# A fp32 decoder trunk: the last output product of an FFN chunk in two halves, no short products, and unused products in TensorE's first two stops

## The chip, the cores and the metric

The kernel runs on one core of one Trainium2 chip. The metric is the device time of one execution in microseconds (us). TensorE (PE) multiplies and loads its stationary operand with a separate instruction (PEld in the rows); VectorE is DVE, ScalarE is ACT, GpSimd is POOL, and SyncE (SP) issues the DMAs.

## The reference

Two layers over 256 tokens of width 1024 in float32: a recurrent layer with an FFN, then shared keys and values and an attention layer with an FFN.

```python
for layer in range(DEPTH):
    if layer < N_A_LAYERS:
        h = h + recurrent_block(h, ...)        # z = rmsnorm(h) @ w_in; conv, gates, scan; @ w_out
    else:
        if layer == N_A_LAYERS:
            shared = shared_kv(h, ...)
        h = h + nsa_layer(h, ..., *shared)
    h = h + swiglu(h, f_norm[layer], f_w_in[layer], f_w_out[layer])

def swiglu(h, norm_g, w_in, w_out):
    u = rmsnorm(h, norm_g)
    gu = u @ w_in
    return (jax.nn.silu(gu[..., :FFN_HIDDEN]) * gu[..., FFN_HIDDEN:]) @ w_out
```

FFN_HIDDEN is 2816.

## The kernel before

Every large product is done in three: each operand is split into a high part and a low part, and `mm3` adds high x high, high x low and low x high into one PSUM bank. Weights come as a stream of 512 KB tiles (`raw`). ACT casts a tile to its high part `wh`, then DVE (now and then POOL) subtracts to get the low part `wl`; when `wl` is written, SP issues the load of the tile four places later.

**The opening.** The order of work in the recurrent layer is written out by hand in `PLAN_A`: each word runs one step of a named piece. PE first runs three unused products (`warm_up`, into the bank `wps`) and a broadcast of the norm's gain (g). `norm_rows` (na) makes a normalised token block on ACT, POOL and DVE; `norm_tr` (nt) transposes it on PE (ntpa), eight 128x128 transposes for each of the two token blocks, and ACT and DVE split the result into `uah` and `ual`. Then come the projections z, each of 24 products of 256 columns: eight with `wh` and `uah`, eight with `wl`, eight with `ual`. `conv` (c) turns each z into a row block X on DVE, whose queue also holds the short steps of `decay` (sp, word d).

**The FFN.** `ffn` works through eleven chunks of 256 hidden units. Chunk 0 is done token-major in `in_mm`. For the chunks 1 to 10 `in_fm(c)` computes gate and up (f0g and f0u; f1g and f1u in the second layer) from four weight tiles, with 256 tokens as moving columns: 96 products of 128x256. `act_fm` makes the hidden values, and `out_both(c-1)` adds the chunk before to the four output banks accf: 2 weight tiles x 2 token blocks x 2 column halves x 3 = 24 products of 128x512. The last two chunks' outputs are done in `out_mm`. So PE goes from 512-column to 256-column products at the start of each `in_fm`, ten times a layer, and there `in_fm` has one product more, `T.matmul(ps[0][:, 0, :LEAD[layer]], ...)`, with 64 columns in the first layer and 96 in the second. The real first product starts its bank anew, so nothing reads it. By the order of instructions it is also the one that waits for ACT's `wh`.

Of the kernel before, what the change touches and what calls it, by code (L numbers as in the profile page):

```python
# [18 lines left out]
P = 128  # L19
# [3 lines left out]
NT = S // P  # L23
# [33 lines left out]

WARM = 3, 0

LEAD = 64, 96  # L60

PLAN_A = """
na0tA na0G na0 na0 nt0A na1 na1 e0t nt0 na1G na1t nt0 nt0tV nt0 w0A nt1a nt1G nt1 nt1a nt0a e0 nt1t nt1 w1 w1 w2 w3
w2V w0G z0V c0 d0 d0 d0 d0 c0 d0G d0 c0G d0 d0A w3G c0 z1 d0 d0 d0 c1 c1 c1a c1G d0 d0 d0 d0 z2 d0V d0a d0 w4 g0 g0 w4
g1G g1 g1 d0 d0 c2 c2 c2 d0 d0 d0 g0 d0 c2 d0 d0 d0 d0 z3 c3 d0 w5 g2 d0 d0 g2 g2 d0 d0 c3a c3A d0 c3 w6 z4 w6 c4 g3
g3 w7 d0V d0 g3 d0A d0 d0 d0 w5G d0 c4 d0 d0 c4 c4 w7 z5 g4 g4 g4 d0 d0 d0 d0 d0 d0 d0 d0 c5 c5 c5 d0 l0 w8 w8G z6 d0
# [150 lines left out]
def hybrid_trunk(ctx: ExitStack, tc: tile.TileContext, x, wsrc, gatew, gains, vecs, cvec, hvec, rope_c, rope_cc,  # L217
                 masks, sel, posT, w2d, out):
    nc = tc.nc
    V, A, T, GP = nc.vector, nc.scalar, nc.tensor, nc.gpsimd  # L220
# [11 lines left out]
    def bank(tag, name):  # L232
        tag = {"m": "mm", "a": "acc", "t": "tp"}.get(on.bank, tag)
        return psum.tile([P, 512], F32, tag=tag, name=name, bufs={"mm": 2, "acc": 4, "tp": 2}[tag])

    def gain(i):
        g = work.tile([P, D], F32, tag="gain", name=f"gain{i}", bufs=1)
        nc.sync.dma_start(g, gains[i:i + 1, :].broadcast_to([P, D]))
        return g[:, 0:512], g[:, 512:1024]
# [13 lines left out]
    for t in range(NT):  # L253
        for i in range(2):
            c = slice(i * 512, (i + 1) * 512)
# [9 lines left out]
    wps = bank("mm", "warmps").rearrange("p (a b) -> p a b", b=P)[:, 0:2]  # L265
# [10 lines left out]
    ident = msk[:, 0:128]  # L276
# [14 lines left out]
    def tok(a, k, t):  # L291
        return a[:, k, t * P:(t + 1) * P]

    def u_tiles(nm, use="m"):
        return [work.tile([P, KT, S], F32R, tag=f"{use}{c}", name=f"u{c}{nm}", bufs=1) for c in "hl"]

    def acc_pair(nm):
        return [bank("acc", f"acc{nm}_{n}") for n in range(2)]
# [42 lines left out]
            V.tensor_tensor(ul, pv, f32v(uh), ALU.subtract)  # L341
            yield

    def mm3(ps, ah, al, bh, bl, start, stop):

        T.matmul(ps, ah, bh, start=start, stop=False)  # L346
        T.matmul(ps, ah, bl, start=False, stop=False)  # L347
        T.matmul(ps, al, bh, start=False, stop=stop)  # L348


    ap = ExitStack()
# [19 lines left out]
    ab, e, z, z2, acc, r0, c2, nc2 = (sp[:, i, :] for i in range(8))  # L371

    def decay():

        V.tensor_scalar(z, e, 2.0, None, ALU.add)
        yield
        V.reciprocal(r0, z)
        yield
        V.tensor_tensor(z, e, r0, ALU.mult)
        yield  # L380
        V.tensor_tensor(z2, z, z, ALU.mult)
        yield
        V.tensor_scalar(acc, z2, 1.0 / 17.0, None, ALU.mult)
        yield
        for k in (15, 13, 11, 9, 7, 5, 3):
            V.scalar_tensor_tensor(acc, acc, 1.0 / k, z2, ALU.add, ALU.mult)
            yield
        V.scalar_tensor_tensor(acc, acc, 1.0, z, ALU.add, ALU.mult)
        yield
        V.tensor_scalar(r0, lam, -1.0, 0.0, ALU.mult, ALU.max)  # L390
        yield
        V.scalar_tensor_tensor(acc, acc, 2.0, r0, ALU.mult, ALU.add)
        yield
        V.tensor_scalar(c2, acc, 2.0, None, ALU.mult)
        yield
        V.tensor_scalar(nc2, acc, -4.0, None, ALU.mult)
        yield

    def consts():
# [70 lines left out]
    def proj_k(t, base, ah, al, ps, k):  # L470
        h, lo = W.parts[base + k]
        for n in range(2):
            c = slice(n * 512, (n + 1) * 512)
            mm3(ps[n], tok(ah, k, t), tok(al, k, t), h[:, c], lo[:, c], k == 0, k == KT - 1)
# [16 lines left out]
    def a_gain():  # L491
        gf0.append(gain(1))
        u0.extend(u_tiles("f0"))
        yield

    do = {
        "na": lambda t: norm_rows(t, g0, f"a{t}"), "nt": lambda t: norm_tr(t, (uah, ual), f"a{t}"), "e": lambda _: consts(),
        "d": lambda _: decay(), "w": lambda *n: W.pieces(), "z": z_mm, "c": conv, "g": gates, "l": lru, "y": y_out,
        "o": a_proj, "r": a_res, "nf": a_tr, "gf": lambda _: a_gain(),
    }  # L500
    play(PLAN_A, do, on)
    ap.close()
# [3 lines left out]
    def ffn(layer, u, wi, mid, fin, more=None):  # L506
# [3 lines left out]
        acc = [None, None]  # L510
# [4 lines left out]
        def in_base(c):  # L515
            return wi if c == 0 else wi + 4 + 6 * (c - 1)

        def out_base(c):
            return in_base(c + 1) + 4 if c < FC - 1 else end - 2

        def in_mm(t, c, late=None):
            ps = bank("mm", f"f{layer}i{t}_{c}")
            for k in range(KT):
                if late and k == KT - 1:
                    late()
                h, lo = W.get(in_base(c) + k // 2)
                s = slice((k % 2) * 512, (k % 2 + 1) * 512)
                mm3(ps, tok(u[0], k, t), tok(u[1], k, t), h[:, s], lo[:, s], k == 0, k == KT - 1)
            return ps
# [11 lines left out]
        def tr(t, c):  # L541
            pt = bank("tp", f"f{layer}t{t}_{c}")[:, :256]
            hd = hid.pop((t, c))
            for k in range(2):
                T.transpose(pt[:, k * P:(k + 1) * P], hd[:, k * P:(k + 1) * P], ident)
            if c not in hT:
                hT[c] = parts(c)
            hh, hl = (tok(m, slice(0, 2), t) for m in hT[c])
            pv = pt.rearrange("p (k q) -> p k q", k=2)
            A.copy(hh, pv)  # L550
            V.tensor_tensor(hl, pv, f32v(hh), ALU.subtract)

        def in_fm(c, between=()):

            tag = "mm" if c % 2 else "tp"
            ps = [bank(tag, f"f{layer}{x}_{c}").rearrange("p (k s) -> p k s", k=2) for x in "gu"]
            for j in range(4):
                h, lo = W.get(in_base(c) + j)
                if j == 0:
                    T.matmul(ps[0][:, 0, :LEAD[layer]], h[:, :P], u[0][:, 0, :LEAD[layer]], start=True, stop=True)  # L560
                for k in range(KT):
                    s = slice(k * P, (k + 1) * P)
                    mm3(ps[j // 2][:, j % 2], h[:, s], lo[:, s], u[0][:, k], u[1][:, k], k == 0, k == KT - 1)
                if j < len(between):
                    between[j]()
            return ps
# [28 lines left out]
        def out_both(c):  # L595
            if c == 0:
                for t in range(NT):
                    acc[t] = acc_pair(f"f{layer}_{t}")
            hh, hl = hT.pop(c)
            for k in range(2):  # L600
                h, lo = W.get(out_base(c) + k)
                for t in range(NT):
                    for n in range(2):
                        s = slice(n * 512, (n + 1) * 512)
                        mm3(acc[t][n], tok(hh, k, t), tok(hl, k, t), h[:, s], lo[:, s], c == 0 and k == 0, False)


        with tc.manual_schedule():
            ps = in_mm(0, 0, mid)
            act(0, 0, ps)  # L610
            W.split(wi + 6)
            ps = in_mm(1, 0)
            act(1, 0, ps)
        for c in range(1, FC - 1):
            W.split(in_base(c) + 4)
            ps = in_fm(c, [lambda: tr(0, 0), lambda: tr(1, 0)] if c == 1 else ())
            act_fm(c, ps)
            out_both(c - 1)
            if c == 1 and more:
                more()  # L620
        c = FC - 1
        W.split(end)
        ps = in_fm(c)
        act_fm(c, ps)
        for t in range(NT):
# [15 lines left out]
    w2 = pt1.tile([P, 2, 2, HD], F32, name="w2")  # L641
# [34 lines left out]
    ps = {}  # L676
# [567 lines left out]
```

## Time and profile before

| | us |
|---|---|
| median of 3 runs | 627.31 (627.07 to 627.53) |
| the profiled execution | 628.81 |
| its span, first to last instruction | 626.8 |
| PE busy | 611.4 (98%) |
| PE loading stationary operands | 548.2 (87%) |
| DVE busy | 407.7 (65%) |
| ACT busy | 327.0 (52%) |
| POOL busy | 117.9 (19%) |

The durations of single instructions overlap on PE: products are pipelined, and a product of 0.39 us may be followed by the next after 0.23. What a product costs in a run is therefore the step from its start to the next one's start. The clock column is the granted share of TensorE's full speed; an idle time in square brackets is that of the engine before the row, with what ended it.

### The profile page before, as it was taken

The numbers are of one execution on the slowest core, as the hardware profiler recorded it, in microseconds if no ns is written. First come the engines' busy times: TensorE is split into PE (matmuls) and PEld (weight loads), VectorE is DVE, ScalarE is ACT, GpSimd is POOL, SyncE is SP. The second block draws the span as 40 slices with busy tenths as digits, with TensorE's granted clock in tenths as the row PEclk, the third lists the DMA queues.
The fourth block names the chain that finished last, engine by engine and source line by source line (L and its number), as shares of the span: only waits on it lengthen the run. The fifth ranks groups of instructions, "written<-read, shape, count | busy, mean of one in ns | idle before, by whom it ended". The sixth has DMA issues, their size and how long they took to land.

```text
span 626.8 us, 10483 instructions
## 1 busy us (share of the span) xinstructions
PE 611.4 (98%) x4087; PEld 548.2 (87%) x4087; DVE 407.7 (65%) x630; ACT 327.0 (52%) x598; POOL 117.9 (19%) x133
## 2 busy tenths in 40 slices
PE   6999899999999999999999999999999999999997
PEld 4899777999999999988999886777899999999996
DVE  5879957755555555559776788888665555555542
ACT  6489656554444444452545578764554444444440
POOL 4223021210000000000446758754100000000000
PEclk8999999999999999999999999999999999999999
DMA  7444563875555655535545340333476666656622
GB/s 274 170 137 167 174 229 122 276 267 195 198 186 187 201 191 185 197 103 182 172 134 183 121 135 7 116 115 106 133 265 202 187 189 198 194 183 196 199 70 67
DMA packets 31380, 106.75 MB, mean 170 GB/s; under 512 B 4014, under 2 KB 5730, under 8 KB 31203
## 3 DMA queue, kind: packets, MB, share of 16 engines
q1 hardware_dynamic: 31331, 106.08, 52.0%
q8 instruction: 32, 0.52, 0.3%
q14 instruction: 17, 0.14, 0.1%
HBM read 105.02 MB, written 1.05 MB: 169 GB/s over the span
## 4 chain that ended last, share of the span: by engine, by line
PE 84%; DVE 7%; ACT 4%; DMA 3%; issue 2%; SPq 0%; DVEq 0%; ACTq 0%
PE accf L348 6%; PE accf L347 6%; PE accf L346 6%; PE f0g L346 3%; PE f1g L346 3%; PE f0g L347 3%; PE f1u L346 3%; PE f0g L348 3%; PE f1g L347 3%; PE f1g L348 3%; PE f0u L347 3%; PE f0u L346 3%; PE f0u L348 3%; PE f1u L347 3%; PE f1u L348 3%; DMA raw<-in_wsrc_dram 3%
## 5 line engine op out<-in xcount | busy, mean ns | idle before, releaser
L204 DVE TENSOR_TENSOR wl<-raw,wh 128x1024 fp32r<-128x1024 f32 x148 | 181.3, 1229 | 137.0 <-ACT wh L143 137.0
L143 ACT CAST wh<-raw 128x1024 fp32r<-128x1024 f32 x161 | 168.1, 1051 | 176.4 <-issue 38.8
L347 PE MATMUL accf<-wl,fhh 128*128 128x512 f32 x176 | 68.6, 390 | 0.0
L348 PE MATMUL accf<-wh,fhl 128*128 128x512 f32 x176 | 68.5, 389 | 0.0
L346 PE MATMUL accf<-wh,fhh 128*128 128x512 f32 x176 | 68.5, 389 | 0.0
L204 POOL TENSOR_TENSOR wl<-raw,wh 128x1024 fp32r<-128x1024 f32 x16 | 40.2, 2518 | 44.1 <-ACT wh L143 20.5
L346 PE MATMUL f0g<-uhf,wh 128*128 128x256 f32 x160 | 45.3, 283 | 0.0
L346 PE MATMUL f1g<-uhf,wh 128*128 128x256 f32 x160 | 45.0, 281 | 0.0
L347 PE MATMUL f0g<-ulf,wh 128*128 128x256 f32 x160 | 44.3, 277 | 0.0
L346 PE MATMUL f0u<-uhf,wh 128*128 128x256 f32 x160 | 44.3, 277 | 0.0
L346 PE MATMUL f1u<-uhf,wh 128*128 128x256 f32 x160 | 44.3, 277 | 0.0
L348 PE MATMUL f0g<-uhf,wl 128*128 128x256 f32 x160 | 44.2, 277 | 0.0
L347 PE MATMUL f1g<-ulf,wh 128*128 128x256 f32 x160 | 44.2, 276 | 0.0
L348 PE MATMUL f1g<-uhf,wl 128*128 128x256 f32 x160 | 44.2, 276 | 0.0
L347 PE MATMUL f0u<-ulf,wh 128*128 128x256 f32 x160 | 44.2, 276 | 0.0
L347 PE MATMUL f1u<-ulf,wh 128*128 128x256 f32 x160 | 44.2, 276 | 0.0
L348 PE MATMUL f0u<-uhf,wl 128*128 128x256 f32 x160 | 44.2, 276 | 0.0
L348 PE MATMUL f1u<-uhf,wl 128*128 128x256 f32 x160 | 44.2, 276 | 0.0
L348 PEld LDWEIGHTS accf<-wh,fhl 128*128 128x128 f32 x176 | 33.0, 188 | 7.0
L347 PEld LDWEIGHTS accf<-wl,fhh 128*128 128x128 f32 x176 | 33.0, 188 | 6.2
L346 PEld LDWEIGHTS accf<-wh,fhh 128*128 128x128 f32 x176 | 33.0, 188 | 6.2
L1019 ACT ACTIVATE pr<-s,sm 128x128 f32<-128x128 f32 (+1 forms) x64 | 26.2, 424 | 9.7 <-DVE sm L1013 6.9
(315 smaller groups left out, 1508.2 us busy)
## 6 DMA issues: line engine op xcount, KB each, us to landing
raw<-in_wsrc_dram SPq DMA_DIRECT2D x184, 512.0 KB, 4.2
raw<-in_wsrc_dram SPq DMA_DIRECT2D x8, 544.0 KB, 4.4
hres<-in_x_dram SPq DMA_DIRECT2D x4, 256.0 KB, 3.2
gw<-in_gatew_dram SPq DMA_DIRECT2D x1, 1024.0 KB
gain<-in_gains_dram SPq DMA_DIRECT2D x2, 512.0 KB, 7.0
out_dram<-hres SPq DMA_DIRECT2D x8, 128.0 KB, 1.8
tab<-in_hvec_dram SPq DMA_DIRECT2D x1, 256.0 KB, 5.0
tab<-in_rope_c_dram SPq DMA_DIRECT2D x1, 128.0 KB, 3.9
```

The costliest lines, as they stand in the source:

```text
L143: self.nc.scalar.copy(dst, src)
L204: self.on.pick(nc.gpsimd if i in LOW_ON_POOL else nc.vector).tensor_tensor(lo[:, :w], t[:, :w], f32v(h[:, :w]), ALU.subtract)
L346: T.matmul(ps, ah, bh, start=start, stop=False)
L347: T.matmul(ps, ah, bl, start=False, stop=False)
L348: T.matmul(ps, al, bh, start=False, stop=stop)
L1019: A.activation(pr[:, h1 + i, br], sv[:, br], AF.Exp, bias=sm[:, 0, h0 + i, br:br + 1], accum_out=sm[:, 1, h0 + i, br:br + 1])
```

## The change

Three edits. `LEAD` and the unused product in `in_fm` are gone. `mm3` can issue its third product (low x high) in two halves of 256 columns, and `out_both` asks for that in the last of its eight `mm3` (k = 1, last token block, second column half). A new piece `fill` (word wm) issues unused products into `wps`; the plan has two of them behind the first block's transposes and three behind the second's. `ident` is the 128x128 identity that the transposes use.

```diff
-LEAD = 64, 96
-
 PLAN_A = """
-na0tA na0G na0 na0 nt0A na1 na1 e0t nt0 na1G na1t nt0 nt0tV nt0 w0A nt1a nt1G nt1 nt1a nt0a e0 nt1t nt1 w1 w1 w2 w3
+na0tA na0G na0 na0 nt0A na1 na1 e0t nt0 wm2 na1G na1t nt0 nt0tV nt0 w0A nt1a nt1G wm3 nt1 nt1a nt0a e0 nt1t nt1 w1 w1 w2 w3
...
-    def mm3(ps, ah, al, bh, bl, start, stop):
+    def mm3(ps, ah, al, bh, bl, start, stop, halves=False):
...
-        T.matmul(ps, al, bh, start=False, stop=stop)
+        for i in range(2 if halves else 1):
+            c = slice(i * 256, (i + 1) * 256) if halves else slice(0, ps.shape[-1])
+            T.matmul(ps[:, c], al, bh[:, c], start=False, stop=stop)
...
+    def fill(n):
+
+        for _ in range(n):
+            T.matmul(wps, ident, ident[:, None, :].to_broadcast([P, 2, P]), start=True, stop=True)
+        yield
...
-        "o": a_proj, "r": a_res, "nf": a_tr, "gf": lambda _: a_gain(),
+        "o": a_proj, "r": a_res, "nf": a_tr, "gf": lambda _: a_gain(), "wm": fill,
...
-                if j == 0:
-                    T.matmul(ps[0][:, 0, :LEAD[layer]], h[:, :P], u[0][:, 0, :LEAD[layer]], start=True, stop=True)
...
-                        mm3(acc[t][n], tok(hh, k, t), tok(hl, k, t), h[:, s], lo[:, s], c == 0 and k == 0, False)
+                        ops = acc[t][n], tok(hh, k, t), tok(hl, k, t), h[:, s], lo[:, s], c == 0 and k == 0, False
+                        mm3(*ops, halves=(k, t, n) == (1, NT - 1, 1))
```

PE's queue before, from the end of one `out_both` to the start of the next `in_fm` (accf are the output banks, wh and wl the weight tile's parts, fhh and fhl the hidden values' parts, uhf and ulf the input's parts):

```order
504 L346 MATMUL accf_1_1_1310<-wh_1531,fhh_1_1293 128x512
505 L347 MATMUL accf_1_1_1310<-wl_1532,fhh_1_1293 128x512
506 L348 MATMUL accf_1_1_1310<-wh_1531,fhl_1_1294 128x512
507 L560 MATMUL f0g_1573<-uhf_867,wh_1549 128x64 [waits Activation_49]
508 L346 MATMUL f0g_1573<-uhf_867,wh_1549 128x256
509 L347 MATMUL f0g_1573<-ulf_868,wh_1549 128x256
```

and the same place after the change:

```order
504 L345 MATMUL accf_1_1_1314<-wh_1535,fhh_1_1297 128x512
505 L346 MATMUL accf_1_1_1314<-wl_1536,fhh_1_1297 128x512
506 L349 MATMUL accf_1_1_1314<-wh_1535,fhl_1_1298 128x256 x2
507 L345 MATMUL f0g_1578<-uhf_872,wh_1554 128x256 [waits Activation_49]
508 L346 MATMUL f0g_1578<-ulf_873,wh_1554 128x256
```

The 64-column product is gone, its wait on ACT has moved to the first real f0g product, and the last accf product stands as two of 256 columns.

PE's queue before in the opening, from the gain's broadcast to the first z (msk holds the identity, xna the normalised tokens):

```order
3 L274 MATMUL g_101<-grow,zero 128x512
4 L334 MATMUL ntpa_0_133<-msk,xna_126 128x128 x4
5 L334 MATMUL ntpa_1_134<-msk,xna_126 128x128 x4
6 L334 MATMUL ntpa_0_160<-msk,xna_140 128x128 x4
7 L334 MATMUL ntpa_1_161<-msk,xna_140 128x128 x4
8 L417 MATMUL z_194<-uha,wh_157 128x256 x8
```

and after the change:

```order
3 L272 MATMUL g_101<-grow,zero 128x512
4 L332 MATMUL ntpa_0_133<-msk,xna_126 128x128 x4
5 L332 MATMUL ntpa_1_134<-msk,xna_126 128x128 x4
6 L403 MATMUL warmps<-msk 128x256 x2
7 L332 MATMUL ntpa_0_162<-msk,xna_140 128x128 x4
8 L332 MATMUL ntpa_1_163<-msk,xna_140 128x128 x4
9 L403 MATMUL warmps<-msk 128x256 x3
10 L424 MATMUL z_199<-uha,wh_159 128x256 x8
```

Two unused products stand behind the first block's transposes and three behind the second's. The queues of ACT, DVE, POOL and SP are as before.

## Rows read from the trace of the kernel before

**Rows 1.** The page: the chain that ended last, shares of the span

```profile
PE 84%; DVE 7%; ACT 4%; DMA 3%; issue 2%; SPq 0%; DVEq 0%; ACTq 0%
```

**Rows 2.** Both FFNs' stretches, in order: length, busy of PE, PEld, DVE, ACT, POOL; clock; DMA

```profile
109.00:264.00 155.00, 155.00 (x1148) 146.40 (x1148) 85.93 (x98) 71.85 (x98) 6.20 (x16) 1.00 0.63 209
...
452.00:623.00 171.00, 171.00 (x1241) 160.21 (x1239) 89.63 (x108) 73.59 (x101) 0.00 (x0) 1.00 0.58 180
```

**Rows 3.** The opening by stretches, columns as in rows 2

```profile
6.14:7.18 1.04, 0.00 (x1) 0.04 (x1) 1.04 (x2) 0.63 (x3) 0.28 (x2) 1.00 0.99 179
...
8.25:9.30 1.05, 0.00 (x0) 0.00 (x0) 0.80 (x2) 0.67 (x2) 1.05 (x2) 1.00 0.95 359
...
10.61:11.15 0.54, 0.01 (x1) 0.00 (x0) 0.00 (x0) 0.42 (x1) 0.00 (x0) 1.00 1.04 432
11.15:12.31 1.16, 0.00 (x0) 0.00 (x1) 0.02 (x1) 1.16 (x3) 0.46 (x1) 0.52 0.99 417
```

**Rows 4.** Timeline of PE in the opening: start, length, instruction, count [idle before <-releaser]

```profile
1.23 2.93 PE L269 MATMUL warmps<-zero 128*128 128x256 f32 x6 [1.23 <-POOL euler L365]
...
9.30 1.31 PE L334 MATMUL ntpa<-msk,xna 128*128 128x128 f32 x8 [1.06 <-DVE xna L326]
12.31 2.08 PE L417 MATMUL z<-uha,wh 128*128 128x256 f32 x8 [1.69 <-ACT uha L143]
...
18.87 1.07 PE L417 MATMUL z<-uha,wl 128*128 128x256 f32 x8
```

**Rows 5.** The chain of waits in the opening: start, length, what

```profile
12.31 5.78 PE z L417 x24
...
29.45 1.10 PE gt L432 x4
```

**Rows 6.** Timeline of PE and its loads where f0g follows accf

```profile
158.83 0.39 PE L348 MATMUL accf<-wh,fhl 128*128 128x512 f32 x1
...
159.06 0.19 PE L560 MATMUL f0g<-uhf,wh 128*128 128x64 f32 x1
159.06 0.19 PEld L346 LDWEIGHTS f0g<-uhf,wh 128*128 128x128 f32 x1
...
159.17 0.19 PEld L347 LDWEIGHTS f0g<-ulf,wh 128*128 128x128 f32 x1
...
159.52 0.28 PE L346 MATMUL f0g<-uhf,wh 128*128 128x256 f32 x1
159.52 0.19 PEld L347 LDWEIGHTS f0g<-ulf,wh 128*128 128x128 f32 x1
```

**Rows 7.** The same in the second FFN, PE alone, with 96 columns

```profile
600.79 0.39 PE L348 MATMUL accf<-wh,fhl 128*128 128x512 f32 x1
...
601.48 0.28 PE L346 MATMUL f1g<-uhf,wh 128*128 128x256 f32 x1
```

**Rows 8.** Timeline of PE in the attention part, s behind v

```profile
345.81 0.39 PE L348 MATMUL v<-wh,ulkv 128*128 128x512 f32 x1
346.03 0.28 PE L1001 MATMUL s<-kh,qTh 128*128 128x256 f32 x1
...
346.39 0.28 PE L1001 MATMUL s<-kh,qTh 128*128 128x256 f32 x1
```

**Rows 9.** Timeline of PE within one run of f0g

```profile
161.57 0.28 PE L346 MATMUL f0g<-uhf,wh 128*128 128x256 f32 x1
...
161.91 0.28 PE L346 MATMUL f0g<-uhf,wh 128*128 128x256 f32 x1
```

**Rows 10.** Timeline of PE: the first two gates' products

```profile
23.40 1.02 PE L432 MATMUL gt<-X,gw 128*128 128x256 f32 x4
```

**Rows 11.** Timeline of POOL and DVE in the opening

```profile
11.85 2.39 POOL L204 TENSOR_TENSOR wl<-raw,wh 128x1024 fp32r<-128x1024 f32 x1 [1.77 <-ACT wh L143]
...
14.09 2.37 DVE L204 TENSOR_TENSOR wl<-raw,wh 128x1024 fp32r<-128x1024 f32 x2
...
18.12 0.54 DVE L422 TENSOR_SCALAR X<-z,vec 128x256 f32<-128x256 f32 x1 [1.66 <-PE z L417]
```

## The prediction

> **What bounds the kernel now.** I read the page's chain first: what ended last lies on TensorE (PE) for 84% of the span [rows 1]. The table by stretches then shows where that share is firm. In both feed-forward (FFN) stretches PE is busy without a gap, 155.00 of 155.00 us and 171.00 of 171.00 us, with the clock at 1.00, while in the first of them DVE works 85.93 us and ACT 71.85 us [rows 2]. What leaves PE's row there leaves the end of the kernel too, since the engines that prepare its operands have 40% to spare. The opening is different. PE stands still from 8.25 to 9.30 and from 10.61 to 12.31 us, and within the second of these stops its granted clock falls from 1.00 to about half (1.2 instead of 2.4 GHz) [rows 3, 4]. The first product group z of the recurrent layer then takes 5.78 us in the chain of waits [rows 5]; later eights of the same product take 1.07 us each, so the clock is full again by 18.87 [rows 4]. DVE, which turns z into X, stood idle 1.66 us for it [rows 11].
>
> **Part one: the short products.** Where an FFN changes from 512-column products (accf, and once per layer f0i or f1i) to 256-column ones (f0g, f1g), the kernel before issues one unused product of 64 or 96 columns: chunks 1 to 10 of two layers, 20 places. At one of them the last accf product starts at 158.83, the unused one at 159.06, and the fourth real one at 159.52 [rows 6]. The loads say why: the load for the first real product starts beside the unused one at 159.06, the load after it at 159.17. A load thus holds the next product back for 0.11 us, however short the unused one is. With 96 columns it is as long: from 600.79 to 601.48 [rows 7], 0.69 us as from 158.83 to 159.52.
>
> What a place costs without the unused product stands elsewhere in the trace. In the attention part a 512-column product v is followed directly by 256-column products s, into another bank and, by the order of instructions, behind a wait on ACT, as at the FFN's places. From the last v at 345.81 to the fourth s at 346.39 it takes 0.58 us [rows 8]. Removal is worth 0.69 - 0.58 = 0.11 us, and 20 x 0.11 = **2.2 us**, on a stretch of PE without gaps. Nothing covers it, and nothing is late next by these rows.
>
> **Part two: the halves.** At 18 of the 20 places (nine chunks in each of two layers; the two behind f0i and f1i stay) the last 512-column product comes as two of 256 columns: 18 products and 18 loads more. In the 512-column run products stand 0.23 us apart [rows 6]; in the 256-column run three steps take 161.91 - 161.57 = 0.34, so 0.113 each [rows 9], and two halves take what one whole did. Right behind 512-column products the steps are longer: 346.03 to 346.39 is three steps in 0.36, 0.12 each [rows 8], and two halves take 0.24. I take this, as it is the same situation: 18 x 0.01 = **+0.2 us**. The ends are 0 (long-run steps) and 0.02 a place, 0.4 in all.
>
> A rule of the Trainium skill speaks against this part. The rows first: the load that starts at 159.52 runs beside the product that starts at 159.52 [rows 6], and a run of such pairs goes on at 0.113 us each [rows 9]. "TensorE: Matmul & The Clock Gate", section "The mechanism" of its part on packing, says that LDWEIGHTS overlaps with running MATMULs only when the row group differs; all loads here use the whole array, so by it each added load would stand uncovered, and the sum would be that of rival (2). The trace does not agree: 0.113 us per pair leaves no room for an uncovered load of 0.11.
>
> **Part three: the fills.** Five unused products of 128x256 fp32 go into PE's queue, two behind the first token block's transposes and three behind the second's. The warm-up has the same shape: three such products are six instructions and take 2.93 us at the start of the program [rows 4]. At full clock the gate products, of this shape too, take 1.02 us for four instructions [rows 10]. With the clock up, two fills take about 1.0 us in a stop of 1.05, and three about 1.5 us in a stop of 1.70. Neither delays what follows, whose releasers are DVE and ACT [rows 4]. No other engine's queue changes, and no DMA is added or moved.
>
> What they buy: the stops at 8.25 and 10.61 are nearly closed, and I expect the clock to stay at 1.00, as it did through the single stop from 6.14 to 7.18 [rows 3]. Then z's first eight products end at 12.31 + 1.07 = 13.4. The second eight still wait for wl, which POOL ends at 11.85 + 2.39 = 14.24 [rows 11], and start at 14.3 as now. The 16 that are left take 16 x 0.113 = 1.81 us, and the last one's tail is 1.07 - 8 x 0.113 = 0.17, so z ends near 16.3 and not at 12.31 + 5.78 = 18.09. What is late next is DVE itself: its two wl run to 14.09 + 2.37 = 16.46. X can begin at 16.48 and not at 18.12 [rows 11]: **1.64 us** earlier. From there the chain is DVE's up to 29.45 [rows 5], so the gain goes on; the weights of the next groups are prepared by ACT, DVE and POOL in their queues, and a load is issued when a wl frees its buffer, so the loads behind z move along. The ends of this term: 0 if the clock falls anyway (a rival below), 0.8 if half of it is lost to a load or to ACT on the way, 1.8 if all of z's gain counts (18.09 - 16.3).
>
> **Sum.** -2.2 + 0.2 - 1.64 = -3.64 us, against the profiled execution's 628.81 us (its span 626.8 and 2.0 around it): 625.2. That execution is 1.50 us above the median of the runs, so for the median it is 627.31 - 3.64 = **623.7 us**. The forecast's own range, with 0.10 to 0.12 for a place, 0 to 0.4 for the halves, 0.8 to 1.8 for the clock and 0.2 for the spread of the times before: 622.9 to 625.1. About 0.2%, 1.25 us, is what a measurement here can tell from no change.
>
> **Rivals.**
> (1) The clock falls anyway: the stop from 6.14 remains, the one before wl (13.4 to 14.3) is new, and between the fills there are transposes alone. Then z takes its 5.78 us, the fills cost nothing, and 2.2 - 0.2 is left: 625.3 us. For it: two rounds of transposes between the stops did not keep the clock up [rows 3, 4]. It would also be the result if the timed executions never lost the clock, for which the 1.50 us between profile and median speaks a little. Against it: PE stands still for about 0.2 us between 7.18 and 13.4, where it stood 2.7. "TensorE: Matmul & The Clock Gate", section "Part 4: PE-mode transpose", says that transposes do not count as PE-busy in the same way; the fall behind two rounds of them agrees with it. Chance 0.21.
> (2) The halves' loads are not hidden: 18 x 0.11 = 2.0 us back instead of 0.2, so 625.5 us. The steps of the 256-column run speak against it. Chance 0.04.
> (3) The clock is at half when the fills run. At the warm-up's price two take 2.93 x 2 / 3 = 1.95 us and three 2.93: the transposes come 0.9 us late, and z 1.2 us after that. If z stays slow too, 2.1 us is lost and the FFNs' 2.0 is eaten: 627.4 us. Against it: the clock is 1.00 at 8.25 and at 10.61 [rows 3]. Chance 0.03.
> (4) Slower. The first f0g product now carries the wait on ACT that the unused one carried. If a waiting load does not start beside the product before it, a place shows that product's whole 0.28 us and a load's whole 0.19 us [rows 6] instead of a step of 0.11: 0.36 more, 20 x 0.36 = 7.2 us, and 623.7 + 7.2 = 630.9 us. It decides from 3.64 / 20 = 0.18 us a place. Against it: the s product at 346.03 has such a wait and starts 0.22 us after the v before it [rows 8]; in the order of instructions a chunk's second weight tile is waited for in mid-run as well, and PE's row has no gap [rows 2]. Chance 0.04.
>
> **How the numbers follow.** The forecast gets 0.68; the rivals have 0.21, 0.04, 0.03 and 0.04. Faster: 0.68 + 0.21 + 0.04 = 0.93; same 0.03; slower 0.04. The range takes the forecast's lower end and reaches over (1) to 625.5; (3), (4) and the tails stay out.
>
> **What would show it.** Part one: no step above 0.24 us between the last accf product and the first f0g products, and each chunk 0.1 us shorter. Part two: the two accf halves start 0.11 to 0.12 apart, with one load each. Part three: the clock stays at 1.00 from 8 to 20 us, z ends near 16.3 and X starts near 16.5. I am wrong if a gap opens before the first f0g product, or if z still takes 5.8 us. If X starts early and the recurrent layer ends when it did, a weight load or ACT held the gain.

## The result, and the profile after

The change makes the kernel faster: 624.00 us in the median of five runs (623.06 to 625.14) against 627.12 (626.72 to 627.53) for the kernel before. The ratio is 0.9937, with an interval of [0.9911, 0.9964]. The same kernel timed again later (r_after below) gave 625.09 against 627.13, ratio 0.9963 [0.9945, 0.9980]. The forecast was 623.7 with a range from 622.9 to 625.5, and faster at 0.93.

The profiled execution took 624.92 us, its span 622.9, against 628.81 and 626.8. The page of the kernel after, the shares of the chain that ended last:

```profile
PE 85%; DVE 7%; ACT 4%; DMA 2%; issue 2%; DVEq 0%; ACTq 0%
```

Little moves on the page: PE still makes the chain, 85% where [rows 1] has 84%. It is the stages that show where the 3.97 us of span went. The first product of each stage starts at these times, read from the two timelines of PE:

| us from the span's start | before | after | difference | of which in the stage before |
|---|---|---|---|---|
| f0i, the first FFN's first chunk | 96.64 | 94.68 | -1.96 | -1.96 (opening, recurrent layer) |
| acckc, behind the first FFN | 281.08 | 277.97 | -3.11 | -1.15 (first FFN) |
| f1i, the second FFN's first chunk | 438.00 | 435.03 | -2.97 | +0.14 (attention) |
| end of the span | 626.84 | 622.87 | -3.97 | -1.00 (second FFN) |

So these two executions differ in two places: by about 2 us in the opening, and by 2.15 us in the two FFNs. The second difference belongs to the kernels. The first belongs in part to the executions: r_before_a, a second profile of the kernel before, reached f0i at 93.49, earlier than the 94.68 here. Between it and the second profile of the kernel after, r_after, with f0i at 93.49 and 93.64 and spans of 624.11 and 622.15, the FFNs' gain is all that is left.

**The opening.** PE's timeline after (start, length, instruction, count [idle before]), to lay beside [rows 4]:

```profile
8.29 1.77 PE L332 MATMUL ntpa<-msk,xna 128*128 128x128 f32 x8
9.90 1.03 PE L403 MATMUL warmps<-msk 128*128 128x256 f32 x4
10.89 1.32 PE L332 MATMUL ntpa<-msk,xna 128*128 128x128 f32 x8
12.04 1.46 PE L403 MATMUL warmps<-msk 128*128 128x256 f32 x6
13.15 1.28 PE L424 MATMUL z<-uha,wh 128*128 128x256 f32 x8
14.28 1.07 PE L424 MATMUL z<-uha,wl 128*128 128x256 f32 x8
15.18 1.07 PE L424 MATMUL z<-ula,wh 128*128 128x256 f32 x8
```

The fills are the two rows warmps, 1.03 us for two and 1.46 for three, and no row from 8.29 on has an idle time. Two stretches in the table by stretches (length, busy PE, PEld, DVE, ACT, POOL; clock; DMA):

```profile
9.53:13.15 3.62, 3.62 (x22) 2.84 (x22) 2.95 (x5) 3.42 (x6) 3.58 (x3) 1.00 1.02 425
13.15:20.00 6.85, 6.85 (x61) 6.82 (x60) 6.71 (x12) 3.69 (x4) 3.35 (x2) 1.00 0.70 242
```

PE does not stand at all from 8.29 to 13.15, where it stood 2.7 us before, and the clock is 1.00 from 9.53, where this trace's record of it begins. (The table counts time without a record as 1.00. Ahead of 9.53 it was still at half by the steps: the first four transposes from 8.29 on start 0.21 us apart, those from 9.57 on 0.11.) In [rows 3] it is 0.52 ahead of z. The last row of z begins at 15.18 and takes 1.07, so z ends at 16.25; DVE's own two wl run from 14.01 to 16.36, and its first X starts behind them without a wait, at 16.29 and not at 18.12 [rows 11]:

```profile
16.29 0.54 DVE L429 TENSOR_SCALAR X<-z,vec 128x256 f32<-128x256 f32 x1
```

**The FFNs.** One place and the next in the first FFN, PE's timeline after, beside [rows 6]; then the end of the run of 256-column products between them:

```profile
140.15 0.40 PE L349 MATMUL accf<-wh,fhl 128*128 128x256 f32 x2
140.38 0.29 PE L345 MATMUL f0g<-uhf,wh 128*128 128x256 f32 x1
...
151.28 0.39 PE L345 MATMUL accf<-wh,fhh 128*128 128x512 f32 x1
...
156.74 0.29 PE L345 MATMUL f0g<-uhf,wh 128*128 128x256 f32 x1
```

The two halves start at 140.15 and the next product at 140.38: 0.23 us for both. The chunk's period is 156.74 - 140.38 = 16.36 us. Before it was 16.47 (the short product at 159.06 in [rows 6], the next at 175.53):

```profile
175.53 0.19 PE L560 MATMUL f0g<-uhf,wh 128*128 128x64 f32 x1
```

From chunk 2 to chunk 10 a layer has eight such periods, which agree within 1 ns: 16.473 before and 16.360 after in the first FFN, 16.460 and 16.360 in the second. (The period of chunk 1, which also holds transposes, is longer.) The second profiles of both kernels, r_before_a and r_after, have the same periods, so the experiments on the FFNs are read from periods, which tell 0.01 us a chunk apart, and the timed runs stand beside them.

### The profile page after: what moved, and what is told of

It is laid out like the page before. It is cut to its first block, busy times and chain, and to the rows that moved or that the text cites. A ratio compares the mean times of both kernels' runs of the same rounds, so it can differ in the third digit from the quotient of the medians.

```text
span 622.9 us, 10494 instructions
## 1 busy us (share of the span) xinstructions
PE 610.3 (98%) x4095; PEld 546.2 (88%) x4095; DVE 407.6 (65%) x630; ACT 327.4 (53%) x598; POOL 117.8 (19%) x133
## 4 chain that ended last, share of the span: by engine, by line
PE 85%; DVE 7%; ACT 4%; DMA 2%; issue 2%; DVEq 0%; ACTq 0%
PE accf L346 6%; PE accf L349 6%; PE accf L345 6%; PE f0g L349 3%; PE f1g L349 3%; PE f0u L349 3%; PE f0g L345 3%; PE f1g L345 3%; PE f1g L346 3%; PE f1u L349 3%; PE f0g L346 3%; PE f1u L346 3%; PE f0u L345 3%; PE f1u L345 3%; PE f0u L346 3%; DVE wl L202 2%
## 5 line engine op out<-in xcount | busy, mean ns | idle before, releaser
L349 PE MATMUL accf<-wh,fhl 128*128 128x512 f32 (+1 forms) x194 | 68.7, 369 | 0.0
L349 PEld LDWEIGHTS accf<-wh,fhl 128*128 128x128 f32 x194 | 36.4, 188 | 7.7
```

Source lines behind the costliest of these rows:

```text
L349: T.matmul(ps[:, c], al, bh[:, c], start=False, stop=stop)
```

## The experiments

Two questions were open: which of the three edits gives what, and why the places cost what they cost. All kernels compute the reference's outputs; where one has unused products more or fewer than the kernel before or after, they are work whose result nothing reads.

### The parts apart

**e1_fills**: the kernel before with the fills alone.

```diff
+def fill(n):
+    for _ in range(n):
+        T.matmul(wps, ident, ident[:, None, :].to_broadcast([P, 2, P]), start=True, stop=True)
+    yield
...
-na0tA na0G na0 na0 nt0A na1 na1 e0t nt0 na1G na1t nt0 nt0tV nt0 w0A nt1a nt1G nt1 nt1a nt0a e0 nt1t nt1 w1 w1 w2 w3
+na0tA na0G na0 na0 nt0A na1 na1 e0t nt0 wm2 na1G na1t nt0 nt0tV nt0 w0A nt1a nt1G wm3 nt1 nt1a nt0a e0 nt1t nt1 w1 w1 w2 w3
```

> The kernel before with the five fills alone: the short products stay, the last output product stays whole. My theory (the opening is worth some 1.6 us and does not depend on the FFNs): 1.2 to 1.9 us under the kernel before, z ends near 16.3 us, the clock is 1.00 up to 20 us, and an FFN chunk still takes 16.47 us. Rival (timed executions rarely lose the clock, so the gain in the profile is not one in the times): the profile shows the early X, the times stand within 0.5 us of before.

Measured: 626.12 us against 626.65, ratio 0.9985 [0.9965, 1.0004]. The clock of the profiled execution does not fall, X starts at 15.09 and the span is 623.6. The timed gain, 0.5 us, is not to be told from nothing. It is much less than the 2 us between the two profiles above and than the 1.2 to 1.9 that I expected; the rival, that timed executions rarely lose the clock, fits better.

**e2_no_short**: the kernel before without the short products, nothing else.

```diff
-                if j == 0:
-                    T.matmul(ps[0][:, 0, :LEAD[layer]], h[:, :P], u[0][:, 0, :LEAD[layer]], start=True, stop=True)
```

> The kernel before without the short products, nothing else: no fills, no halves. My theory (a short product costs a load's 0.11 us, and the change from 512 to 256 columns costs nothing by itself): 2.0 to 2.3 us under the kernel before, a chunk takes 16.36 us. Rival (the change of width costs by itself, and the halves are what removes it): 1 us or less under before, and a step over 0.24 us at the first f0g products.

Measured: 634.38 us against 626.65, ratio 1.0106 [1.0063, 1.0149]: slower. Part of it is another matter: three of its six executions had a mean clock of 0.992 or less, and in the profiled one of these the clock fell for about 10 us in the middle of the kernel (below). The other three took 631.56, 632.08 and 632.51, some 5.4 us above 626.65. Neither the theory nor the rival had expected a loss. The period shows why. PE's timeline of e2 at two places in a row:

```profile
140.40 0.39 PE L349 MATMUL accf<-wh,fhl 128*128 128x512 f32 x1
140.62 0.28 PE L345 MATMUL f0g<-uhf,wh 128*128 128x256 f32 x1
...
157.37 0.28 PE L345 MATMUL f0g<-uhf,wh 128*128 128x256 f32 x1
```

Nothing stands between 140.40 and 140.62, and the first real product follows in 0.22 us. Yet the period is 157.37 - 140.62 = 16.75 us, against 16.47 with the short product. Taking the short product away alone costs 0.27 us a chunk.

**e4_no_halves**: the kernel after with a whole last product, so fills and no short products.

```diff
-                        mm3(*ops, halves=(k, t, n) == (1, NT - 1, 1))
+                        mm3(*ops, halves=False)
```

> The changed kernel with the last output product whole again: fills, and no short products. My theory: within 0.3 us of the changed kernel (624.0), so 3 to 3.7 us under before, a chunk takes 16.36 us as with halves. Rival (halves carry it): 1 us or more slower than the changed kernel.

Measured: 630.41 us against 626.65, ratio 1.0064 [1.0034, 1.0094]. PE's timeline of e4 at the same place, the end of the run and the next place:

```profile
139.02 0.39 PE L349 MATMUL accf<-wh,fhl 128*128 128x512 f32 x1
139.25 0.28 PE L345 MATMUL f0g<-uhf,wh 128*128 128x256 f32 x1
...
150.44 0.28 PE L349 MATMUL f0u<-uhf,wl 128*128 128x256 f32 x1
150.56 0.39 PE L345 MATMUL accf<-wh,fhh 128*128 128x512 f32 x1
...
156.00 0.28 PE L345 MATMUL f0g<-uhf,wh 128*128 128x256 f32 x1
```

This is the main reading of the study. The period is again 156.00 - 139.25 = 16.75. The 96 products of the chunk run from 139.25 to 150.56, 11.31 us or 0.118 each; after the change they run from 140.38 to 151.28, 10.90 us or 0.1135 each. The loss is not at the place: the place only decides at which of two rates the whole run goes. At 0.118 every product of the run, the last too (150.44 to 150.56), stands 0.12 behind the one before.

**e3_short_halves**: the kernel before without the short products and with the halves, no fills.

```diff
-                    T.matmul(ps[0][:, 0, :LEAD[layer]], h[:, :P], u[0][:, 0, :LEAD[layer]], start=True, stop=True)
...
-        T.matmul(ps, al, bh, start=False, stop=stop)
+        for i in range(2 if halves else 1):
+            c = slice(i * 256, (i + 1) * 256) if halves else slice(0, ps.shape[-1])
+            T.matmul(ps[:, c], al, bh[:, c], start=False, stop=stop)
...
-                        mm3(acc[t][n], tok(hh, k, t), tok(hl, k, t), h[:, s], lo[:, s], c == 0 and k == 0, False)
+                        ops = acc[t][n], tok(hh, k, t), tok(hl, k, t), h[:, s], lo[:, s], c == 0 and k == 0, False
+                        mm3(*ops, halves=(k, t, n) == (1, NT - 1, 1))
```

> The kernel before without the short products and with the halves, without fills. My theory: 1.8 to 2.3 us under before, within 0.3 us of the run without halves, since two halves take 0.233 us where the whole took 0.227 to 0.236. Rival (the halves carry the gain): more than 1 us faster than the run without short products alone.

Measured: 625.40 us against 626.65, ratio 0.9980 [0.9955, 1.0004], 1.25 us less where the periods give 2; the interval holds both, and also no change. The periods are those of the kernel after: two runs start at 142.24 and 158.60, 16.36 us apart. So without the short product the halves are needed: its removal costs 0.27 a chunk, they give 0.39 back, and 0.11 is left. The halves with the short product kept were not run.

### What sets the rate of a run

The first theory was that a run of 256-column products entered from a regular run of 512-column ones goes into the slow rate, and that anything that breaks the step there sets the fast one. The short product would be such a break, and the halves another one that costs nothing. A rival was that only a 256-column product of another bank counts, or the place of the wait on ACT.

**g1_lead256**: e4 with an unused 256-column product in front of each run.

```diff
+                if j == 0:
+                    T.matmul(ps[0][:, 0], h[:, :P], u[0][:, 0], start=True, stop=True)
```

> The changed kernel with whole output products and instead an unused product of 256 columns ahead of each f0g and f1g run: as many 256-column products behind the last 512-column one as with halves less one, but into f0g's own bank and with f0g's own weights. Theory (a 256-column product directly behind 512-column ones starts a slow run, whatever it computes): chunks of 16.86 us, 16.75 and 0.118. Rival (one more 256-column product is enough to set the fast rhythm): 16.47 us.

PE's timeline of g1 at one place and the next (the row of L567 is the unused product):

```profile
139.40 0.28 PE L567 MATMUL f0g<-uhf,wh 128*128 128x256 f32 x1
...
156.29 0.28 PE L567 MATMUL f0g<-uhf,wh 128*128 128x256 f32 x1
```

156.29 - 139.40 = 16.89, a whole run at 0.118 plus one more product; 633.39 us against 627.13, ratio 1.0091 [1.0046, 1.0135]. The first real product no longer carries the wait, and the run stays at 0.118. So neither the wait nor an unused product as such sets the rate: the short product worked by being short.

**g3_384_128**: the last 512-column product cut into 384 and 128 columns.

```diff
-            c = slice(i * 256, (i + 1) * 256) if halves else slice(0, ps.shape[-1])
+            c = slice(i * 384, min(384 + i * 384, 512)) if halves else slice(0, ps.shape[-1])
```

> The changed kernel with the last output product in 384 and 128 columns, not twice 256. Theory (any product that breaks the step of 0.227 us sets the fast rhythm; 128 columns make the next product wait for its load, as the short product did): chunks of about 16.41 us, that is 16.36 and some 0.05 for the load that 128 columns do not cover. Rival (only 256-column products behind one another into the same bank do it): chunks of 16.75 us as without halves.

PE's timeline of g3 at one place and the next:

```profile
139.24 0.33 PE L345 MATMUL f0g<-uhf,wh 128*128 128x256 f32 x1
...
155.65 0.33 PE L345 MATMUL f0g<-uhf,wh 128*128 128x256 f32 x1
```

155.65 - 139.24 = 16.41: the fast rate, and 0.05 us a chunk that this cut loses at the place itself. Timed, 625.04 us against 627.13, ratio 0.9970 [0.9946, 0.9994].

**g2_halves_early**: the halves in the first of the last `mm3`'s three products, the two behind them whole.

```diff
-        T.matmul(ps, ah, bh, start=start, stop=False)
-        T.matmul(ps, ah, bl, start=False, stop=False)
         for i in range(2 if halves else 1):
             c = slice(i * 256, (i + 1) * 256) if halves else slice(0, ps.shape[-1])
-            T.matmul(ps[:, c], al, bh[:, c], start=False, stop=stop)
+            T.matmul(ps[:, c], ah, bh[:, c], start=start, stop=False)
+        T.matmul(ps, ah, bl, start=False, stop=False)
+        T.matmul(ps, al, bh, start=False, stop=stop)
```

> The changed kernel with the two halves one mm3 product triple earlier in place: the first of the last three products is in halves, the two behind it are whole. Theory (the step just ahead of the run decides, and two whole products of 0.227 us bring it back): slow runs, chunks of 16.75 us. Rival (halves anywhere in the last triple keep the fast rhythm): 16.36 us.

PE's timeline of g2 at one place and the next (the first row holds the halves):

```profile
137.73 0.40 PE L347 MATMUL accf<-wh,fhh 128*128 128x256 f32 x2
137.96 0.40 PE L348 MATMUL accf<-wl,fhh 128*128 128x512 f32 x1
138.20 0.40 PE L349 MATMUL accf<-wh,fhl 128*128 128x512 f32 x1
138.43 0.28 PE L347 MATMUL f0g<-uhf,wh 128*128 128x256 f32 x1
...
154.81 0.28 PE L347 MATMUL f0g<-uhf,wh 128*128 128x256 f32 x1
```

My theory fell here. Two whole products stand between the halves and the run, as regular as the others, and the period is still 154.81 - 138.43 = 16.38; 624.28 us against 626.58, ratio 0.9970 [0.9947, 0.9994]. What differs is the step of the 512-column products themselves: by the trace's unrounded times the two of them start 0.233 and 0.236 us ahead of the next one, where those ahead of a run at 0.118 stand 0.227 apart. The 512-column products also have two steps, and in these kernels a run of 256 columns entered from them directly was fast behind the longer one and slow behind the shorter one.

The direct change from f1i to f1g, where no kernel here but g4 has halves, agrees. After the change the last 512-column product stands 0.24 ahead of f1g and the run is fast; in e3, with the same code there, 0.22 and slow. First after, then e3, PE's timeline:

```profile
449.12 0.40 PE L349 MATMUL f1i<-wh,ulf 128*128 128x512 f32 x1
449.36 0.28 PE L345 MATMUL f1g<-uhf,wh 128*128 128x256 f32 x1
...
450.05 0.28 PE L345 MATMUL f1g<-uhf,wh 128*128 128x256 f32 x1
```

```profile
450.83 0.39 PE L349 MATMUL f1i<-wh,ulf 128*128 128x512 f32 x1
451.05 0.28 PE L345 MATMUL f1g<-uhf,wh 128*128 128x256 f32 x1
...
452.00 0.28 PE L349 MATMUL f1g<-uhf,wl 128*128 128x256 f32 x1
```

After: six steps from 449.36 to 450.05, 0.115 each, the first ones longer. In e3: eight steps from 451.05 to 452.00, 0.119 each. At that place the rate differs from kernel to kernel, and it was the fast one in after, r_after and g2, the slow one in e2, e3, e4, g1, g3 and k1.

**k1_mid_short**: e4 with a 64-column unused product in the middle of a run that goes at 0.118, into the other bank, ahead of the thirteenth product.

```diff
+                    if j == 0 and k == 4:
+                        T.matmul(ps[1][:, 0, :64], h[:, s], u[0][:, k, :64], start=True, stop=True)
```

> Fills, whole last output products, and the unused 64-column product not ahead of each f0g and f1g run but behind its first twelve products. Theory (the rhythm is a state of the run that one short product's wait for a load switches, wherever it stands): twelve products at 0.118 us, the rest at 0.113, a chunk of 16.36 + 12 x 0.0044 + 0.115 = 16.53 us. Rival (the rhythm belongs to the place where the run begins): slow throughout, 16.75 + 0.115 = 16.86 us.

PE's timeline of k1 through the start of one chunk (the row of L569 is the short product):

```profile
157.25 0.28 PE L345 MATMUL f0g<-uhf,wh 128*128 128x256 f32 x1
...
158.54 0.28 PE L349 MATMUL f0g<-uhf,wl 128*128 128x256 f32 x1
158.66 0.19 PE L569 MATMUL f0u<-uhf,wh 128*128 128x64 f32 x1
...
159.48 0.28 PE L345 MATMUL f0g<-uhf,wh 128*128 128x256 f32 x1
159.82 0.28 PE L345 MATMUL f0g<-uhf,wh 128*128 128x256 f32 x1
```

Ahead of it eleven steps take 158.54 - 157.25 = 1.29, 0.117 each; behind it three take 159.82 - 159.48 = 0.34, 0.113 each, and the run stays there. One short product switches a run that is on its way. The period is 16.53, as expected: twelve products at the slow rate and the rest at the fast one. But it does not only switch to the fast rate. In chunk 1 of the first layer the run of k1 starts fast, and the same short product makes it slow (f0t are two transposes that stand there in every kernel):

```profile
107.60 0.28 PE L349 MATMUL f0g<-uhf,wl 128*128 128x256 f32 x1
...
108.28 0.28 PE L349 MATMUL f0g<-uhf,wl 128*128 128x256 f32 x1
108.39 0.19 PE L569 MATMUL f0u<-uhf,wh 128*128 128x64 f32 x1
...
108.62 0.28 PE L346 MATMUL f0g<-ulf,wh 128*128 128x256 f32 x1
...
109.80 0.28 PE L349 MATMUL f0g<-uhf,wl 128*128 128x256 f32 x1
109.92 0.38 PE L552 MATMUL f0t<-msk,fhid 128*128 128x128 f32 x2
...
110.95 0.28 PE L346 MATMUL f0g<-ulf,wh 128*128 128x256 f32 x1
...
112.77 0.28 PE L349 MATMUL f0g<-uhf,wl 128*128 128x256 f32 x1
```

Six steps ahead of it take 108.28 - 107.60 = 0.68, 0.113 each, and ten behind it 109.80 - 108.62 = 1.18, 0.118 each; behind the two transposes the run is fast again, 16 steps in 112.77 - 110.95 = 1.82. So in mid-run the short product changed the rate, 19 times to the fast one and once to the slow one. Timed, 627.91 us against 626.58, ratio 1.0016 [0.9998, 1.0033].

**g4_halves_all**: the kernel after with halves also ahead of the two runs behind f0i and f1i.

```diff
-            T.matmul(ps[:, c], al, bh[:, c], start=False, stop=stop)
+            T.matmul(ps[:, c], al, bh[:, c], start=False, stop=stop and (i == 1 or not halves))
...
-                mm3(ps, tok(u[0], k, t), tok(u[1], k, t), h[:, s], lo[:, s], k == 0, k == KT - 1)
+                mm3(ps, tok(u[0], k, t), tok(u[1], k, t), h[:, s], lo[:, s], k == 0, k == KT - 1, t == NT - 1 and k == KT - 1)
```

> The changed kernel, with the last product of chunk 0's second input projection (f0i, f1i) in two halves as well, so that all 20 places have them. Theory (the halves decide the rhythm): both first f0g and f1g runs at 0.113 us a product, 0 to 0.8 us under the changed kernel, more often 0 since its own two direct places were fast in its profile. Rival (the rhythm there is set by the steps before, which differ): one of the two runs slow as in the run without fills.

Both first runs are fast, and the first periods of both layers are 16.93, as in the kernel after, whose first runs were fast too; where the first run was slow (e2 and e4, second layer) they are 17.11. Timed, 624.52 us against 627.13, ratio 0.9952 [0.9927, 0.9978]; r_after on the same chip has 0.9963 [0.9945, 0.9980]. The measurement does not tell the two apart.

### What the fills are worth

**r_after** is the kernel after again, **r_before_a** one more profile of the kernel before: does the clock fall in each of its executions?

> The changed kernel once more, beside the kernel before on the same chip and in the same call as the next runs. Theory now (of 256-column products a run of f0g keeps one of two rhythms, 0.113 or 0.118 us a product, and directly behind whole 512-column products at 0.227 us it falls into the slow one): chunks of 16.36 us as in its first profile, 2 to 3 us under the kernel before.

> The kernel before once more, for a second profile of its opening. Theory now (its clock falls in the opening in some executions alone): if the clock stays up, z's last sixteen products take 0.113 us each, X starts 1.5 to 2 us earlier than 18.12 and the span is 1 to 2 us under 626.8; if it falls, as in its first profile. Rival (the fall comes in every execution): the clock is at half in the opening again.

Measured: r_after has the result above; its clock does not fall and X starts at 15.33. In r_before_a the clock does not fall either, without any fill. Its table by stretches, and then PE's timeline:

```profile
9.00:11.00 2.00, 1.48 (x9) 1.01 (x10) 1.89 (x4) 1.93 (x4) 1.96 (x2) 1.00 1.05 430
11.00:13.00 2.00, 1.47 (x10) 1.13 (x11) 2.00 (x4) 2.00 (x3) 1.71 (x1) 1.00 0.99 420
```

```profile
10.83 1.40 PE L417 MATMUL z<-uha,wh 128*128 128x256 f32 x8
12.76 1.21 PE L417 MATMUL z<-uha,wl 128*128 128x256 f32 x8 [0.53 <-POOL wl L204]
```

Stops there are (1.48 of 2.00 us busy, then 1.47), the clock column says 1.00, and z's first eight products take 1.40 us. X starts at 14.95, earlier than the 16.29 after the change. So the theory held that the clock falls in some executions alone, and the rival fell. The difference is larger than it said: X starts 3.17 us earlier than in the first profile (1.5 to 2 expected), and the span is 2.7 us shorter (1 to 2).

The two executions differ in one thing more. In the first profile ACT waited 1.81 us for a weight tile to land. Its cast of this tile came late, and so did the cast of uha behind it, for which z waits:

```profile
10.73 1.04 ACT L143 CAST wh<-raw 128x1024 fp32r<-128x1024 f32 x1 [1.81 <-DMA raw<-in_wsrc_dram]
```

In r_before_a this cast starts at 9.20 without a wait. The four profiles without fills agree: in before and e3 ACT waited 1.81 and 1.19 us, PE stood 1.69 and 1.19 ahead of z, and the clock fell; in r_before_a and e2 it did not wait, there was no such stop, and the clock stayed. With fills the clock stayed also where ACT waited (0.58 to 0.88 us in g1, g2, g3, k1 and r_after). Whether a late tile is what it takes, four profiles don't show.

How often it does happen, the mean granted clock of each execution tells: the fall in the opening left 0.994 in the first profile of before and 0.997 in that of e3. Of the 94 timed executions without fills (before, e2, e3) 20 stand between 0.993 and 0.997; of the 83 with fills not one does. Where in an execution its clock fell, the mean does not say, but by this count the fills do what they were put in for. What they save is only what a fall costs: the kernel before takes 626.33 us in the median of its 55 executions at full clock and 627.72 in the 15 of that band, 1.4 us more, near the 1.64 of the prediction.

Another fall is not touched by them. 11 of the 94 executions without fills stand at 0.992 or lower, and 6 of the 83 with fills. The profiled execution of e2 shows where, in the table by stretches of the attention part:

```profile
366.00:372.00 6.00, 5.21 (x47) 4.50 (x46) 5.15 (x13) 5.02 (x21) 0.87 (x3) 1.00 0.40 147
372.00:383.00 11.00, 10.69 (x49) 9.92 (x50) 7.04 (x17) 6.35 (x23) 5.81 (x11) 0.53 0.00 0
```

PE is busy for 5.21 of 6 us ahead of it, and the clock then stands at half for some 10 of the 11 us. The kernel before took 632.06 us in the median of its 6 such executions. Why these executions and not others, no run here tells.

## Why the prediction was right, and where it was not

**What bounds the kernel** held: what left PE's row in the FFNs left the end too (-1.15 and -1.00 us), and no engine came late in its place.

**The FFNs' sum held, its two terms did not.** The forecast was -0.11 a place for the short products and +0.01 for the halves. Measured by periods in the first FFN, they are +0.27 (16.75 against 16.47) and -0.39 (16.36 against 16.75). The sum is -0.11 in the first FFN and -0.10 in the second, 2.15 us in all against the 2.0 forecast.

The step that failed is the one from [rows 8] to the price of a place. It took the s products behind v, 0.12 us a step, for what 256-column products do right behind 512-column ones, and [rows 9], 0.113 a step, for what they come to later. From that followed that a place ends after three steps. In fact the two groups show two rates, each of which holds for a whole run, and the run of s is only six products long, too short to tell a transition from a rate. At none of the 20 places did the trace of before show a run without the short product, and so it could not show what the short product did for the run. But it held both rates: in chunk 1 the 24 products from 112.06 on, between two pairs of transposes, go at 0.118, and the 48 behind them at 0.113. That the sum came out rests on luck in this sense: the halves happened to bring the fast rate back. Without them, with the same argument, I would have forecast about 2 us less in the FFNs for a kernel that is 4 to 5 us slower.

**The halves' loads** (rival 2) are hidden: both halves with their loads take 0.23 us as one whole product does. The rule quoted from the Trainium skill, "TensorE: Matmul & The Clock Gate", section "The mechanism", that such loads don't overlap, is not borne out; the same section also lets a load run ahead into a background weight buffer, which the prediction left out.

**The slower rival** (4) put its price on an uncovered load at the wait. That did not happen: the waiting product starts 0.22 to 0.23 us after the one before. But the side it stood for exists: e2 and e4 are slower, by the rate of the run.

**The fills.** In the profiled execution the times came out, but not every step held. The fills took 1.03 and 1.46 us (forecast 1.0 and 1.5), z's second eight started at 14.28 (14.3), z ended at 16.25 (16.3), and X started at 16.29 (16.48), 1.83 us earlier than before (1.64), behind DVE's own wl as forecast. The gain went on: f0i starts 1.96 us earlier. What did not hold is that the fills delay nothing: z started at 13.15, not 12.31. The second stop, into which three fills were to fit, was not there in this execution; ACT had uha's next part ready at 12.17, and z stood behind the fills for about 1 us. It cost next to nothing, since z's second eight had to wait for wl anyway (POOL ends it at 14.10).

What was mis-sized is this term on the median. The working took 1.64 us off an execution that had lost the clock, and then off the median too. The hint stood in rival (1): the profiled execution was 1.50 us above the median of the runs. That fits the lost clock, which the timed runs mostly did not have. By the two groups above the fills save 1.4 us in about a fifth of the executions, in the others nearly nothing; e1, with the fills alone, came out 0.5 us faster, not separable from zero. With 2.15 us from the FFNs, 2.2 to 2.7 us is what the parts explain. The two timings of the whole gave 3.1 and 2.0, so the forecast of -3.64 was about 1 us too large by its mechanism. That the first timing's 624.0 is so near to 623.7 is partly luck; the repeat's 625.09 is nearer to the 625.3 that rival (1) gave for executions that never lose the clock. The fall behind two rounds of transposes, which spoke for that rival, does not decide much: in r_before_a the clock stayed up behind the same transposes. Rival (3), fills at half clock, did not occur, by little: in the profiled execution the record of the full clock begins at 9.53, and the first fill began at 9.90.

## What to carry to other kernels

Before an instruction that does nothing useful is taken out, find out what the instructions behind it do without it, over the whole run and not over three steps: here a 64-column product cost 0.11 us and saved 0.39. A difference of 0.004 us in the step is worth 0.4 us when 96 products follow it, so read steps over long runs, from the first to the last product, and look in the trace of before for runs of the same products at another step. And when the profiled execution is slower than the median, look for what it has that the others may not have (here a clock fall) before a gain from removing that is counted in the median.

## What the runs showed of the hardware

**Two rates of the same run.** 256-column products with a load each run at 0.1135 us (10.90 us for 96) or at 0.118 us (11.31 us for 96), both at full clock, with the same operands, PE without a gap. An unbroken run keeps its rate to the end. Ahead of a run a short product (64 or 96 columns), two halves or a 384 + 128 cut went with the fast rate at every place; a whole 256-column product behind 512-column steps of 0.227 didn't. In mid-run a short product changes the rate, 19 times from slow to fast and once from fast to slow in k1. Two 128-column transposes in chunk 1 change it both ways too, twice in each layer of every profile but in g1's second layer, which stayed at 0.118. The first products of z show both as well: eight take 0.94 us in e1 and in r_before_a, 0.90 after the change. "TensorE: Matmul & The Clock Gate", section "Back-to-back issue gap", of the Trainium skill gives N / 2.4 + 2.5 ns as the gap of products by themselves, 256 / 2.4 + 2.5 = 109 ns here (an estimate), and says that in a stream of loads and products both set the spacing; the trace has two spacings for one column count, both longer than that gap. What inside the chip holds a run at one of them stays open: the load of the next product starts at the same moment in both, and no run here tells more.

**The clock in the opening falls in some executions only**: by the mean clock in about a fifth of those without fills. The stops themselves differ from one execution to another: ahead of z PE stood 1.69 us in [rows 4], where the clock fell from 1.00 to half; in r_before_a there was no such stop, PE was busy for 1.48 and 1.47 of 2.00 us in the two stretches there, and the clock stayed up.
